# Another assignment of 64 KiB chunks to SBUF partitions in the first tile of a row normalization

## The chip, the cores and the metric

The kernel runs on one core of a Trainium2 chip. The metric is the device time of one execution in microseconds (us), a median over several executions. The record marks every run as fast or slow. All timed runs quoted here are fast ones, at full granted clock, save one single run, whose state is unknown because it was alone. Differences of a few tenths of a microsecond matter in this case, so most experiments were timed in five rounds beside the kernel before, on the same chip (experiments 1 to 8 on one chip, 9 to 12 on another). Figures of single packets and landings come from one profiled execution of each kernel.

## The reference

```python
# x: 1024 x 4096 float32, axis = -1, eps = 1e-12
norm = np.sqrt(np.sum(x ** 2, axis=axis, keepdims=True) + eps)
return (x / norm).astype(np.float32)
```

Each row is divided by its length. The input is 16.78 MB and so is the output.

## The kernel before

The 1024 rows form two tiles of 128 partitions with four rows (64 KiB) each. Each tile has a buffer of its own, so both loads are issued at the start (at 0.0 and 0.8 us). The first load's instruction is moved to the very front of the program. Here is the part that matters:

```python
R = 4
n_tiles = N // (P * R)                                   # 2
x_t   = x.rearrange("(t p r) d -> t p (r d)", p=P, r=R)
out_t = out_flat.rearrange("(t p r) d -> t p (r d)", p=P, r=R)
# ...
for i in range(n_tiles):
    g = RowGroups(nc, io, stats, scratch, D, R, eps_t)
    load = nc.sync.dma_start(out=g.flat(), in_=x_t[i])   # 128 x 64 KiB
    if i == 0:
        first_load_to_front(nc, load.ins)
    groups.append(g)

for i, g in enumerate(groups):
    g.square_dve(R - 1)          # sum of squares of row 3 on VectorE
    g.square_act(0)              # rows 0, 1, 2 on ScalarE
    g.norm(0)
    g.scale(0)                   # VectorE, in place
    # ... rows 1 and 3 ...
    g.square_act(2)
    g.norm(2)
    g.scale(2)
    store = nc.sync.dma_start(out=out_t[i], in_=g.flat())
```

## Time and profile before

| what | value | where it is from |
|---|---|---|
| time before the change was seen | 82.73 us, median of 3 (82.72 to 83.13) | timed runs |
| same kernel beside the later experiments | 82.81 to 82.84 us, medians of 11 or 12 | timed runs |
| VectorE and ScalarE busy | 35% and 33% of the span | page, part 1 |
| DMA engines busy | 97.1% | page, part 3 |
| first load lands, second load lands | 21.89 and 41.89 us | landings in the trace |
| first store issued | 37.88 us | timeline |
| last store lands, span ends | 80.58 and 81.13 us | trace |

The transfers are the bound. Beside the page I use the trace's records of single packets, which give start, duration and size. Every 64 KiB chunk is one packet (512 packets of 65,536 bytes). The records don't name the engine, but nearly every packet starts within 0.004 us of the end of another, which gives 16 chains of 32 packets each; I take each chain for one of the page's 16 DMA engines. Packets 1 to 8 of a chain belong to the first load, 9 to 16 to the second load, 17 to 24 to the first store, 25 to 32 to the second. I call what a packet takes beyond 2.418 us its excess. Two groups of packets have one: the first packet of each engine, and packet 16, the last of the second load.

### The profile page before, as it was taken

What the parts mean: (1) busy time and instruction counts of PE and PEld (TensorE: products, weight loads), DVE (VectorE), ACT (ScalarE), POOL (GpSimd) and SP (SyncE); (2) the same over time, 40 slices, a digit from 0 to 9 for tenths busy, and PEclk for the clock granted to TensorE, in tenths of its full rate; (3) what the DMA queues carried; (4) which work ended last, traced back from release to release, by engine and by line L of the source; (5) the groups of instructions that cost most, each with busy time, mean ns of one, the idle gap of its engine ahead of it and who ended that gap; (6) DMA issues with size and microseconds to landing.
All of it is one profiled execution on the core that took longest, in us unless ns stands there. A gap on an engine that the chain in (4) does not pass through costs nothing.

```text
span 81.1 us, 93 instructions
## 1 busy us (share of the span) xinstructions
DVE 28.6 (35%) x21; ACT 26.4 (33%) x22; POOL 0.2 (0%) x4
## 2 busy tenths in 40 slices
DVE  0000000000199599976039995999200000000000
ACT  6000000000199999930039999950000000000000
POOL 0000000000000000000000000000000000000000
DMA  9099999299999759999099995899998399998390
GB/s 517 0 517 517 517 517 485 129 420 517 517 517 485 323 226 517 517 517 517 0 517 517 517 452 226 355 517 517 517 485 388 162 517 517 517 517 388 162 485 0
DMA packets 577, 33.55 MB, mean 414 GB/s; under 512 B 65, under 2 KB 65, under 8 KB 65
## 3 DMA queue, kind: packets, MB, share of 16 engines
q1 hardware_dynamic: 576, 33.55, 97.1%
q14 instruction: 1, 0.00, 0.0%
HBM read 16.78 MB, written 16.78 MB: 414 GB/s over the span
## 4 chain that ended last, share of the span: by engine, by line
DMA 51%; ACT 10%; DVE 9%; issue 0%
DMA xt<-in_x_dram 51%; ACT sq_act L33 9%; DVE xt L64 9%; ACT rstd L53 1%; DVE rstd L59 0%
## 5 line engine op out<-in xcount | busy, mean ns | idle before, releaser
L33 ACT ACTIVATE sq_act<-xt 128x4096 f32<-128x4096 f32 x6 | 21.6, 3608 | 26.5 <-DMA xt<-in_x_dram 26.5
L64 DVE TENSOR_SCALAR xt<-xt,rstd 128x4096 f32<-128x4096 f32 x8 | 18.8, 2353 | 0.3
L42 DVE SCALAR_TENSOR_TENSOR sq_dve<-xt 128x4096 f32<-128x4096 f32 x2 | 8.9, 4426 | 25.0 <-DMA xt<-in_x_dram 25.0
L53 ACT ACTIVATE rstd<-ssq,eps_t 128x1 f32<-128x1 f32 x8 | 2.1, 288 | 0.1
L59 DVE RECIPROCAL rstd<-rstd 128x1 f32<-128x1 f32 x8 | 1.3, 159 | 2.4 <-ACT rstd L53 2.4
L33 ACT ACT_TABLE_LOAD x1 | 1.3, 1283 | 0.8 <-PEq L220 0.8
L53 ACT ACT_TABLE_LOAD x1 | 1.3, 1283 | 0.0
L33 ACT ACTIVATION_READ_ACCUMULATOR sq_act<-xt 128x1 f32 x6 | 1.1, 186 | 0.0
L176 DVE MEMSET eps_t<- 128x1 f32 x1 | 0.1, 59 | 0.9 <-PEq L220 0.9
L42 DVE DVE_READ_ACCUMULATOR sq_dve<-xt 128x1 f32 x2 | 0.2, 83 | 0.0
L220 POOL MEMSET const-uint8-127<- 128x1 uint8 x1 | 0.1, 102 | 0.0
L220 POOL MEMSET const-bfloat16-1.0<- 128x1 bf16 x1 | 0.1, 101 | 0.0
L220 POOL MEMSET const-float32-0.0<- 128x1 f32 x1 | 0.1, 98 | 0.2 <-issue 0.2
L220 POOL MEMSET const-float32-1.0<- 128x1 f32 x1 | 0.1, 98 | 0.0
## 6 DMA issues: line engine op xcount, KB each, us to landing
xt<-in_x_dram SPq DMA_DIRECT2D x2, 31.5
out_dram<-xt SPq DMA_DIRECT2D x2, 23.3
```

What stands on the lines that cost most here:

```text
L33: self.nc.scalar.activation(out=sq_a, in_=self.x[:, r], func=ACT_F.Square, accum_out=self.ssq[:, r : r + 1],)
L42: self.nc.vector.scalar_tensor_tensor(out=sq_v, in0=self.x[:, r], scalar=1.0, in1=self.x[:, r], op0=ALU.mult, op1=ALU.mult, accum_out=self ...
L53: self.nc.scalar.activation(out=self.rstd[:, r : r + n], in_=self.ssq[:, r : r + n], func=ACT_F.Sqrt, bias=self.eps_t,)
L59: self.nc.vector.reciprocal(out=self.rstd[:, r : r + n], in_=self.rstd[:, r : r + n])
L64: self.nc.vector.tensor_scalar_mul(out=self.x[:, r], in0=self.x[:, r], scalar1=self.rstd[:, r : r + 1])
L176: nc.vector.memset(eps_t, eps)
L220: nc = _bacc.Bacc("TRN2", target_bir_lowering=False, num_devices=1)
```

## The change

The intent, as I read it, is to let the DMA engines read neighbouring 64 KiB chunks of HBM at the same time. Only the first tile is regrouped, load and store alike, so the result is the same; the last tile stays in plain order.

```diff
+    B = 4
+    x_f = x.rearrange("(t b g r) d -> t g b (r d)", b=B, g=P // B, r=R)
+    out_f = out_flat.rearrange("(t b g r) d -> t g b (r d)", b=B, g=P // B, r=R)
+    x_v = [x_f[0]] + [x_t[i] for i in range(1, n_tiles)]
+    out_v = [out_f[0]] + [out_t[i] for i in range(1, n_tiles)]
...
-        load = nc.sync.dma_start(out=g.flat(), in_=x_t[i])
+        load = nc.sync.dma_start(out=g.flat(), in_=x_v[i])
...
-        store = nc.sync.dma_start(out=out_t[i], in_=g.flat())
+        store = nc.sync.dma_start(out=out_v[i], in_=g.flat())
```

## The prediction

> **What bounds the kernel now.** I read the page from the top: the engines' busy time first, the slices of the span next, then the transfer queue, then the chain that ended last, and at last the windows view and the trace's single transfer records.
>
> ```profile
> span 81.1 us, 93 instructions
> DVE 28.6 (35%) x21; ACT 26.4 (33%) x22; POOL 0.2 (0%) x4
> ...
> DMA  9099999299999759999099995899998399998390
> ...
> DMA packets 577, 33.55 MB, mean 414 GB/s; under 512 B 65, under 2 KB 65, under 8 KB 65
> ...
> q1 hardware_dynamic: 576, 33.55, 97.1%
> ```
>
> Both compute engines are busy for about a third of the span, while the transfer queue occupies its 16 DMA engines for 97.1% of it. The low digits in the DMA row are no pauses: packets are long and all 16 engines start them nearly together, so a slice that sees no packet begin shows a low digit. Of the 577 packets 65 are tiny (completion marks and one other), so 512 carry data: 33.55 MB / 512 = 65,536 bytes, one 64 KiB chunk (four rows) for each partition and direction. There are four transfers of 128 chunks (two loads, two stores), so each engine moves 8 chunks of each transfer, 32 in all.
>
> The windows view, cut at the stages, says how fast they go (columns: window, its length, busy time of VectorE, ScalarE and GpSimd, clock, DMA share, GB/s):
>
> ```profile
> 4.60:21.60 17.00, 0.00 (x0) 0.00 (x0) 0.00 (x0) 1.00 1.01 436
> ...
> 36.00:41.90 5.90, 1.85 (x1) 0.00 (x0) 0.00 (x0) 1.00 0.96 378
> 41.90:61.00 19.10, 14.23 (x10) 11.87 (x10) 0.00 (x0) 1.00 1.01 439
> ```
>
> 436 GB/s over 16 engines is 27.25 GB/s each, or 2.41 us for a 64 KiB chunk. The single packet records agree: almost every data packet lasts 2.418 to 2.420 us, loads and stores alike, whether compute runs beside it (41.9 to 61.0) or not (4.6 to 21.6).
>
> The timeline shows why compute does not matter. The loads are issued back to back at the start, the first store at 37.88 us, the second at 57.27:
>
> ```profile
> 37.88 19.73 SPq L202 DMA_DIRECT2D out_dram<-xt  x2
> ```
>
> The second load lands at 41.9, so the first store is already queued behind it; the first store lands at 61.2, so the second is queued behind that one. The DMA engines never wait for compute. The chain of waits on the page follows the compute of the last tile, since it goes back from the last store to the instruction that released it. I do not take it as the bound: that store was released about 4 us before its engines were free.
>
> So the time is one engine's 32 packets in a row plus edges. For the engine that ends last, from the packet records: start at 1.20 us; 32 x 2.418 = 77.38; its first packet takes 3.43 instead of 2.42, an excess of 1.01 (over all engines the first packet lasts 2.64 to 3.43, median 3.1, an excess of about 0.7); packets 14 and 15 add 0.05; packet 16, the last of the second load and the one where loading turns into storing, takes 3.10, an excess of 0.68; neighbouring packets overlap by 0.10 in sum. 1.20 + 77.38 + 1.01 + 0.05 + 0.68 - 0.10 = 80.22 us, and the record says 80.24. The last completion comes at 80.58, the span ends at 81.13, and the timed median is 82.73, 1.6 more than the span.
>
> [...]
>
> **The change part by part.** It alters only which 64 KiB chunk of the first tile lives in which partition. Plainly, partition p holds chunk p. Now partition 4g + b holds chunk 32b + g, in the load and in the store alike, so the result is the same. Nothing is added to the compute engines: the same 43 VectorE and ScalarE instructions on the same shapes, with the same waits.
>
> Packets: the HBM side becomes 32 x 4 chunks instead of 128, still in runs of 64 KiB, so 128 packets for each transfer, 0 more. [...]
>
> [...]
>
> What moves is the HBM address. [...]
>
> What that can be worth: of a tile-0 load's 8 packets, seven already take 2.42 us, and so do all 8 of its store. Only the first packet has any excess, median 0.7 us[...]. If denser addresses save a tenth to a third of it, that is 0.07 to 0.23 us on the path, because the queue behind it moves up by as much. The second load, the turn to storing (0.68) and the second store keep their order: 0. Sum: -0.1 us, 82.73 - 0.1, about 82.6 us.
>
> **The rivals.**
> (1) The split over engines breaks[...]: 8 x 2.42 = 19.3 us more for the load and as much for the store, so 102 to 121 us. [...] I give it 4 in 100.
> (2) HBM suffers from the new addresses[...]. A loss of 2% (1.65 us) needs only 1.65 / 16 = 0.10 us a packet, 4%. [...] I give 4 in 100 to a loss over 2%, and some to a loss of a few tenths.
> (3) The first packets become much quicker: all 16 excesses vanish. That is 0.7 to 1.0 us, 81.7 to 82.0, still within 2%. To pass 2% the change would need 1.65 us, and the slowest engine has 1.74 us of excess in all, 0.73 of it in packets that are not touched.
> (4) The first tile lands earlier and compute starts earlier: worth nothing, since the first store waits in the queue behind the second load anyway.
>
> **Range and chances.** The executions before spread from 82.72 to 83.13. With -0.7 as the good end for the first packets and +0.6 for small losses in HBM, 8 times in 10 I expect 82.1 to 83.3, around 82.6. Slower by over 2%: the rivals 1 and 2 together, 0.08. Faster by over 2%: 0.03, for something I have overlooked. Within 2%: 0.89.
>
> **What would show it.** If right, the profile after has 577 packets and 33.55 MB again, near 436 GB/s between the first packets and the landing of the first load, a first load that lands within 0.5 us of 21.9, a first store issued as much earlier or later, and a span within 0.7 us of 81.1. Rival 1 would show as about 218 GB/s in the windows of the first load and of the first store, rival 2 as packets of 2.5 us or more there, rival 3 as a first load that lands before 21.3. I am wrong if packets of the first tile leave 2.42 us by more than 0.1, or if the second load and second store, untouched, change their time.

The forecast's sum was -0.1 us, 82.73 - 0.1, about 82.6 us. The terms come to -0.1 us: 0.07 to 0.23 us off the measured excess of 0.7, where the fraction, a tenth to a third, was my guess (that the addresses read at one moment become denser was not shown), and zeros for the rest. Of rival 1 an estimate is left, that the first tile's packets take twice their measured 2.42 us.

## The result, and the profile after

The changed kernel takes 83.06 us (median of 6, 82.96 to 83.14); the kernel before, with the runs of the same rounds added, 82.97 us (median of 6, 82.72 to 83.13). The ratio is 1.0013 with a 95% interval of 0.9991 to 1.0035. Ratios throughout are the mean time of one kernel's fast runs over that of the other's fast runs of the same rounds, so they are not quite the ratio of the medians quoted. A difference is not shown. But inside the span two things have moved, by 0.5 to 0.75 us each, in opposite directions.

The page of the changed kernel answers line for line:

```profile
span 81.2 us, 93 instructions
DVE 28.6 (35%) x21; ACT 26.4 (33%) x22; POOL 0.2 (0%) x4
...
DMA packets 576, 33.55 MB, mean 413 GB/s; under 512 B 64, under 2 KB 64, under 8 KB 64
q1 hardware_dynamic: 576, 33.55, 96.4%
```

The work is unchanged, to the instruction and the packet (the one packet less is the instruction fetch that happened to fall into the profile before). The windows view of the changed kernel, same cuts as before, same columns:

```profile
4.60:21.60 17.00, 0.00 (x0) 0.00 (x0) 0.00 (x0) 1.00 1.00 432
...
36.00:41.90 5.90, 2.52 (x2) 0.06 (x1) 0.00 (x0) 1.00 1.18 511
41.90:61.00 19.10, 14.23 (x10) 11.87 (x10) 0.00 (x0) 1.00 1.01 436
```

The steady stages run at the same 432 to 439 GB/s. The view books a packet where it starts, so the middle window must not be read as a rate (511 GB/s are 46 packet starts in 5.9 us, where 39 would fit at 436 GB/s); it does say that something between 36 and 42 us has shifted.

Now the issue, that is, the time that SyncE's instruction takes to hand a transfer over. First the loads, the first store and ScalarE's first work on each tile in the timeline of the kernel before (start, duration, engine or queue, line, operation; the two loads are merged in one line; the lines from 37 us on are from the view cut at 37 to 43 us), then in the changed kernel:

```profile
0.00 1.13 SPq L184 DMA_DIRECT2D xt<-in_x_dram  x2
...
21.91 3.62 ACT L33 ACTIVATE sq_act<-xt 128x4096 f32<-128x4096 f32 x1 [19.83 <-DMA xt<-in_x_dram]
...
37.88 0.35 SPq L202 DMA_DIRECT2D out_dram<-xt  x1
41.91 3.62 ACT L33 ACTIVATE sq_act<-xt 128x4096 f32<-128x4096 f32 x1 [6.64 <-DMA xt<-in_x_dram]
```

```profile
0.00 1.67 SPq L191 DMA_DIRECT2D xt<-in_x_dram  x2
...
22.70 3.62 ACT L33 ACTIVATE sq_act<-xt 128x4096 f32<-128x4096 f32 x1 [20.11 <-DMA xt<-in_x_dram]
...
38.67 0.60 SPq L209 DMA_DIRECT2D out_dram<-xt  x1
42.02 3.62 ACT L33 ACTIVATE sq_act<-xt 128x4096 f32<-128x4096 f32 x1 [5.97 <-DMA xt<-in_x_dram]
```

ScalarE starts on the first tile when it has landed: at 22.70 us instead of 21.91, 0.8 later. Yet the second load lands at 42.00 instead of 41.89. The delay of the first load has all but vanished within the second, which the change did not touch. The tile view shows the cost of one issue, shortest / median / longest in ns, before and after:

```profile
L184 SPq DMA_DIRECT2D xt<-in_x_dram x2: 333/358/383, 0.0 to 0.8; - x2
L202 SPq DMA_DIRECT2D out_dram<-xt x2: 344/346/348, 37.9 to 57.3; - x2
```

```profile
L191 SPq DMA_DIRECT2D xt<-in_x_dram x2: 364/512/660, 0.0 to 1.3; - x2
L209 SPq DMA_DIRECT2D out_dram<-xt x2: 354/479/604, 38.7 to 57.4; - x2
```

Of each pair one is still plain (364 and 354 ns). The regrouped one takes 660 ns for the load and 604 ns for the store, where a plain one takes 0.33 to 0.38 us. Its HBM side now has three dimensions, 32 x 4 x 64 KiB, whose first two have steps that can't be merged into one; that this is the reason is what experiment 9 tests.

The packet records put this together. Means over the 16 engines, us; two profiles of each kernel:

| | before | before, again | changed | changed, again |
|---|---|---|---|---|
| first packet begins | 1.18 | 1.18 | 1.67 | 1.59 |
| first packet lasts | 3.10 | 3.06 | 3.26 | 3.40 |
| first packet ends | 4.28 | 4.24 | 4.94 | 4.99 |
| packets 2 to 8 | 2.42 | 2.42 | 2.42 | 2.42 |
| excess of packet 16 | 0.50 | 0.64 | 0.01 | 0.01 |
| last packet of the slowest engine ends | 80.23 | 80.19 | 80.34 | 80.36 |

In the means over the engines, then, the change costs 0.65 to 0.75 us at the front and gets 0.5 to 0.6 us back where loading turns into storing. The question for the experiments is whether either is chance, what causes each, and whether the gain can be had without the cost.

### The profile page after: what moved, and what is told of

It is laid out like the page before. It is cut to its first block, busy times and chain, and to the rows that moved or that the text cites. A ratio compares the mean times of both kernels' runs of the same rounds, so it can differ in the third digit from the quotient of the medians.

```text
span 81.2 us, 93 instructions
## 1 busy us (share of the span) xinstructions
DVE 28.6 (35%) x21; ACT 26.4 (33%) x22; POOL 0.2 (0%) x4
## 4 chain that ended last, share of the span: by engine, by line
DMA 50%; ACT 10%; DVE 9%; issue 0%
DMA xt<-in_x_dram 50%; ACT sq_act L33 9%; DVE xt L64 9%; ACT rstd L53 1%; DVE rstd L59 0%
```

## The experiments

Two theories. (By the record's verdict, which asks for 2%, every kernel below but the one of experiment 4 is the same as the kernel before. Where I call one slower or quicker, the 95% interval of its ratio leaves 1 out.) **Timing**: packet 16 is long in the kernel before because the first store is issued while the second load is still running, and early; the late start of the changed kernel makes the first tile, and hence that store, later, and the stretch goes away. **Address**: packet 16 is short in the changed kernel because the regrouped order suits HBM better. A third theory, **chance**, says that the long packets were an accident of one execution.

### 1 and 2. Both kernels again, unchanged

> The kernel before, unchanged, as its own control. Theory (the change costs about 0.5 us at the first issue and wins back about 0.5 us where loading turns into storing): the last packets of the second load again take 2.8 us or more, the first packets begin at about 1.0 to 1.6 us, ratio 1.000. Rival (the long last packets of the second load, 2.8 to 3.1 us, are chance of one execution): here they last 2.42 to 2.5 us.

> The changed kernel, unchanged, a second profile. Theory: the first load's issue again takes about 0.5 us longer, the first packets begin at 1.45 us or later, and the last packets of the second load stay at 2.42 to 2.45 us; ratio 1.000 to 1.003. Rival (chance): the last packets of the second load are long here, or the start is as early as before.

The kernel before measured 82.76 us against 82.84 for itself, ratio 0.9993 (0.9978 to 1.0008): this is how well the comparison resolves. The changed kernel measured 83.03, ratio 1.0019 (1.0002 to 1.0037). Together with the first comparison, the change makes the kernel slower by perhaps 0.1 to 0.2%. The table above has both repeat profiles: the stretch of packet 16 and the late start are there again in the respective kernel. Chance alone is out for both. It was right for one thing: packets 13 to 15 of the first profile before had 0.14 us of excess in sum, and none in the second.

### 3. The second tile regrouped instead of the first

```diff
-    x_v = [x_f[0]] + [x_t[i] for i in range(1, n_tiles)]
-    out_v = [out_f[0]] + [out_t[i] for i in range(1, n_tiles)]
+    x_v = [x_t[0], x_f[1]]
+    out_v = [out_t[0], out_f[1]]
```

> The regrouping in the second tile alone (load and store), the first tile plain. If the cost is only the issue of the three-dimensional side: the first packets begin at 1.0 to 1.6 us as before, the longer issue of the second load hides behind the first, and the time is that of before (ratio 0.998 to 1.002), or lower by up to 0.6 us (0.993) if the turn from loading to storing is quick as well. If the new addresses themselves cost time in HBM: packets of the second load or store above 2.5 us, ratio above 1.005.

It measured 82.71 us, ratio 1.0000 (0.9978 to 1.0021). The earliest packet begins at 1.02 us as in the kernel before, and the long issue of the second load (648 ns) costs nothing behind the first load. The packets of the regrouped second load and store are at 2.42 us in the steady state. So regrouping costs when it is the first transfer of the program. Packet 16 had an excess of 0.13 us, between the two kernels, although the first store is plain here and was issued 0.28 us before the mean start of packet 16, nearly as in the kernel before (0.34). Timing alone does not give that. But the profiled execution was the fastest of a scattered lot (82.46 to 83.17), and this run alone does not decide between timing and address.

### 4. Groups of eight partitions

```diff
-    B = 4
+    B = 8
```

> As the change, but 16 groups of eight partitions instead of 32 groups of four. [...] the load and the store of the first tile take up to 19.3 us more each (102 to 121 us in all). Rival: [...] time as before, 83 us.

It measured 124.69 us (one run, state unknown, but the slowest of all other kernels is 41 us faster). The first load lands at 43.38 us instead of 22.68 (+20.7), the first store takes 40.4 us after the second load's landing instead of 19.4 (+21.0), and these 41.7 us are the whole difference from 83.03. The windows view, cut inside the first load and the first store:

```profile
5.00:40.00 35.00, 0.00 (x0) 0.00 (x0) 0.00 (x0) 1.00 1.02 210
64.00:100.00 36.00, 12.85 (x10) 10.49 (x10) 0.00 (x0) 1.00 0.99 213
```

All 16 engines are busy (share 1.02 and 0.99) and move 210 and 213 GB/s, about half of 436. The median packet of the first load takes 5.11 us, and so does that of the first store, where single ones scatter from 3 to 6. This is the breakdown that the prediction's first rival describes, built on purpose, with the rate that it was given (about 218 GB/s). Even its size nearly fits: 5.11 us against 2 x 2.42 = 4.84, 5% more. The 32 groups of the change keep each engine at 2.42 us, so whatever slows the 16 groups isn't there. What that is was not shown: the trace doesn't name the partition of a packet. That the new HBM addresses slow the 16 groups is a possibility which no run excludes; against it stands only that the 32 groups, with new addresses too, stayed at 2.42 us a packet.

### 5 and 6. The load alone, the store alone

Each of these mixes a regrouped and a plain side, so the rows come out in the wrong order.

```diff
# e_load_only
-    out_v = [out_f[0]] + [out_t[i] for i in range(1, n_tiles)]
+    out_v = [out_t[i] for i in range(n_tiles)]
# e_store_only
-    x_v = [x_f[0]] + [x_t[i] for i in range(1, n_tiles)]
+    x_v = [x_t[i] for i in range(n_tiles)]
```

> Only the first load is regrouped, the first store is plain (the rows come out in the wrong order on purpose). Both theories expect the late start: first packets at 1.45 us or later. Timing theory (the last packets of the second load are stretched when the first store is issued well before they end): the store is issued at about 38.65 us and those packets stay under 2.5 us, time as the changed kernel, ratio 1.001 to 1.003. Address theory (they are short because the first store writes regrouped addresses): they take 2.8 us or more here, ratio about 1.007.

> Only the first store is regrouped, the first load is plain (wrong order of rows on purpose). Both: first packets at 1.0 to 1.6 us, store issued at about 37.8 us. Timing theory: the last packets of the second load take 2.6 to 3.1 us, a little less than before [...]; ratio 0.997 to 1.001. Address theory: those packets take 2.42 to 2.45 us, ratio about 0.994.

The load alone measured 83.33 us, ratio 1.0052 (1.0031 to 1.0072), with the first packets at 1.41 us or later and 0.11 us of excess in packet 16 (2.42 to 2.87 us). The store alone measured 82.44, ratio 0.9958 (0.9937 to 0.9978), with an early start and 0.03 us of excess. Its timeline:

```profile
37.88 0.64 SPq L209 DMA_DIRECT2D out_dram<-xt  x1
41.25 3.62 ACT L33 ACTIVATE sq_act<-xt 128x4096 f32<-128x4096 f32 x1 [5.99 <-DMA xt<-in_x_dram]
```

The two halves add up: +0.52% from the load and -0.42% from the store give +0.1%, and the whole change measured 0.13% and 0.19%, with intervals of about 0.2% to either side of each. Each theory missed something. With the load alone the excess is mostly gone although the store is plain, against the address theory; but some packets took over 2.5 us and the ratio lies above the 1.001 to 1.003 of the timing theory. With the store alone it is gone although the store was issued at 37.88 us exactly as before, where the timing theory had expected 2.6 us or more. One way out keeps timing: the regrouped store's issue takes 0.64 us instead of 0.35, so although it begins at 37.88 us as before it ends 0.29 us later. The next two runs were made to tell.

### 7 and 8. The plain store later, the regrouped store earlier

```diff
# b_store_late: the kernel before, result right
         g.scale(2)
+        if i == 0:
+            nc.vector.tensor_scalar_mul(out=g.x[:, 2, :1280],
+                                        in0=g.x[:, 2, :1280], scalar1=1.0)
         store = nc.sync.dma_start(out=out_t[i], in_=g.flat())
# a_store_early: the changed kernel, one row in four of tile 0 wrong on purpose
#   (square_act gets a second argument, the number of columns; that edit is cut here)
-        g.square_act(2)
+        g.square_act(2, 3072 if i == 0 else D)
```

> The kernel before, with one more VectorE multiplication by 1.0 over 1280 columns ahead of the first store alone, about 0.8 us; the result is right. Timing theory: the first store is issued at about 38.6 us, the last packets of the second load shrink from 2.9 to about 2.43 us and the end comes 0.5 us earlier, ratio 0.994. Address theory: those packets stay at 2.8 to 3.1 us and the time stays, ratio 1.000.

> The changed kernel with ScalarE's third square of the first tile cut to 3072 of 4096 columns (one row in four of that tile gets a wrong norm on purpose), so that the first store is issued about 0.85 us earlier, at 37.8 us. Timing theory: the last packets of the second load stretch to 2.7 to 3.1 us and the end comes about 0.3 to 0.5 us later than the changed kernel's, ratio to before 1.006. Address theory: they stay at 2.43 us, ratio 1.001 to 1.003.

The kernel before with a useless multiplication of 0.83 us ahead of its first store measured **82.16 us, ratio 0.9920** (0.9903 to 0.9937), with the right result. The timeline of that kernel:

```profile
37.88 0.83 DVE L203 TENSOR_SCALAR xt<-xt 128x1280 f32<-128x1280 f32 x1
38.73 0.35 SPq L204 DMA_DIRECT2D out_dram<-xt  x1
41.21 3.62 ACT L33 ACTIVATE sq_act<-xt 128x4096 f32<-128x4096 f32 x1 [5.95 <-DMA xt<-in_x_dram]
```

More work on the path to the store, a store issued 0.85 us later, and the second load arrives 0.7 us earlier (41.21 against 41.91), because packet 16 lasts 2.43 us on every engine. No address differs from the kernel before. Conversely the changed kernel with its regrouped store issued at 37.86 us has 0.28 us of excess in packet 16 (2.45 to 3.29 us), its second load lands at 42.67, and it takes 83.55 us (median of 4), ratio 1.0093 (1.0075 to 1.0111), more than the 1.006 that was expected. So timing alone is enough to remove the stretch, and regrouped addresses do not wholly prevent it. The address theory falls as the only cause. It is not shown that the regrouping has no part of its own: 0.28 us is less than the plain store's 0.50 and 0.64, though the regrouped store came earlier against packet 16 (0.86 us before its start; plain 0.34 and 0.39).

### 9. Three dimensions without the regrouping

Tile 0 takes every other group of four chunks and tile 1 the rest. Within a group of partitions the chunks are neighbours as in plain order, but each HBM side is 32 x 4 x 64 KiB as in the change.

```diff
-    x_f = x.rearrange("(t b g r) d -> t g b (r d)", b=B, g=P // B, r=R)
+    x_f = x.rearrange("(g t b r) d -> t g b (r d)", b=B, g=P // B, r=R)
# the output likewise; x_v and out_v are x_f and out_f for both tiles
```

> Tile 0 takes every other group of four chunks, tile 1 the rest, in both loads and stores; within a partition group the four chunks are neighbours as in the plain order, but each HBM side is three-dimensional (32 x 4 x 64 KiB) and can't be merged. If the late start comes from the shape of the transfer's HBM side: first load's issue 0.64 to 0.67 us, first packets from 1.4 us, first load lands at 22.4 or later, although no neighbouring chunks are spread over groups. If it comes from the regrouped addresses: issue 0.33 to 0.38, first packets from 1.0 us, landing by 21.9. In time: with the shape, about as the changed kernel, ratio 1.000 to 1.004; with the addresses, 0.994 to 0.998.

It measured 82.80 us, ratio 0.9995 (0.9977 to 1.0012). The tile view of the loads has both of them long now:

```profile
L191 SPq DMA_DIRECT2D xt<-in_x_dram x2: 564/612/660, 0.0 to 1.3; - x2
```

The first packets begin at 1.58 us in the mean, as in the changed kernel (1.59 and 1.67) and not as before (1.18, and 1.18 to 1.30 in all profiles with a plain first load): the late start of 0.4 to 0.5 us comes from the shape of the transfer, not from spreading neighbouring chunks over groups. But the first packet ends at 4.70 us, against 4.91 to 4.99 in the four profiles with the regrouped first load and 4.24 to 4.45 in those with a plain one, and the first load lands at 22.22 us, not at 22.4 or later as expected. So some 0.2 us of the change's cost may belong to the regrouped addresses of the very first packets. That rests on one profile against four. In time this kernel lies at the lower edge of what the shape was expected to cost (1.000 to 1.004); the excess of its packet 16 is 0.10 us.

### 10 to 12. When should the first store be issued?

```diff
# the kernel before, with the added multiplication over
#   320 columns (b_store_bit_late) or 3712 columns (b_store_too_late);
# b_store_early: g.square_act(2, 3072 if i == 0 else D), wrong on purpose
```

> The kernel before with ScalarE's third square of the first tile cut to 3072 of 4096 columns (a wrong norm in one row of four of that tile, on purpose): the first store is issued at about 37.0 us. Timing theory: the last packets of the second load, or the two last, stretch at least as much as before (mean excess of 0.5 us or more an engine), ratio 1.000 to 1.008. Address theory, already hurt: unchanged.

> The kernel before with an added VectorE multiplication over 320 columns (about 0.25 us) ahead of the first store. Timing theory: issue at about 38.1 us, excess of the last load packets between 0.0 and 0.3 us, ratio 0.992 to 0.997. If only a delay of the best part of a microsecond helps: 1.000.

> The same with 3712 columns (about 2.2 us): issue at about 40.1 us[...]. Timing theory: no stretch of the last load packets, but the store's first packets begin at about 41.1 us on all engines instead of 40.3 to 40.8, so the end comes about 0.4 us later than with the delay of 0.8 us: ratio 0.995 to 1.000. If every later issue helps alike: 0.992.

All three came out as the timing theory expected. They were run on another chip. Together with the earlier runs of the plain kernel they give a curve. Packet 16 begins between 38.05 and 38.22 us (mean over engines) in all of them:

| first store issued at | against the mean start of packet 16 | mean excess of packet 16 | first store packet begins, mean | ratio to before |
|---|---|---|---|---|
| 37.05 (early) | -1.04 | 0.93 | 41.45 | 1.0043 |
| 37.66 (before, again) | -0.39 | 0.64 | 41.11 | 0.9993 |
| 37.88 (before) | -0.34 | 0.50 | 41.15 | |
| 38.16 (a bit late) | +0.04 | 0.16 | 40.70 | 0.9955 |
| 38.73 (late) | +0.65 | 0.01 | 40.53 | 0.9920 |
| 40.25 (too late) | +2.12 | 0.01 | 41.16 | 0.9971 |

The excess falls steadily as the store comes later. The last row is the other end: there the excess is zero, but the engines stand idle for 0.6 us in the mean after packet 16, and all start the store together at 41.10 to 41.30 us. Of these times of issue the best is 0.65 us after the start of packet 16.

The curve holds for the plain kernel. Every kernel with something rearranged in groups of four lies below it. Read off in straight lines between the rows (an estimate), the curve gives 0.47 us at the -0.31 of the store alone and of every other group, which had 0.03 and 0.10; 0.85 at the -0.86 of the regrouped store issued early, which had 0.28; and 0.26 and 0.32 at the -0.07 and -0.14 of the changed kernel's two profiles, which had 0.01. The longer issue of a regrouped store (0.60 to 0.64 us against 0.35) may explain a part of that, which was not tested, but not the two kernels whose first store is plain: 0.13 against 0.45 for the second tile (-0.28), 0.11 against 0.33 for the load alone (-0.15). So the later store accounts for about half of what the changed kernel gains at the turn, by this estimate; the rest goes with the regrouping, and the runs do not say by what way.

## Why the prediction was right or wrong

**Right: the bound.** The transfers set the end in every variant, compute ran in their shadow (save that it sets when the first store is issued, see below), and 83.06 us lies in the range and within 2%.

**Right, as far as the trace shows it: the load on the engines, and the steady rate.** 576 packets, 16 chains of 32 data packets again, 432 to 439 GB/s and 2.42 us a packet in the first tile. The argument for it, which partitions an engine serves, was not shown. The breakdown of rival 1 happens at 16 groups and not at 32, at 41.7 us for the two transfers against the 38.6 estimated. Rival 2, HBM suffering in the steady state, did not come about (2.42 us a packet).

**Wrong: "What that can be worth".** The term was -0.1 us from quicker first packets; it measured +0.65 to +0.75. Two things were missed. The change part by part counted compute instructions ("Nothing is added to the compute engines") and packets ("0 more"), and not the price of issuing a transfer: a transfer with an HBM side that cannot be merged takes 0.28 us longer to issue here and brings the first packets 0.4 to 0.5 us later (experiment 9: the shape alone does it). Since this is the first transfer of the program, that is on the path. And the first packets became longer by 0.16 to 0.34, not shorter.

**Wrong: "The second load, the turn to storing (0.68) and the second store keep their order: 0".** The turn went from 0.50 and 0.64 us of mean excess to 0.01, worth -0.5 to -0.6 us. The prediction had seen the long packets, and named them a part that the change doesn't touch, because their addresses stay. It touches them through time: the first load lands 0.8 us later, so the first store comes 0.8 us later, which is worth about half of the gain by the estimate above. The rest, by the same estimate, goes with the regrouping itself: the regrouped store alone, issued at the same 37.88 us, took the excess to 0.03 us. My own condition for being wrong, that the untouched second load changes its time, was met.

**Wrong: "A first load that lands within 0.5 us of 21.9"** (it landed at 22.68) and, in effect, rival 4. It said that an earlier store is worth nothing since it waits in the queue behind the second load. In fact, in the kernel before, an earlier store costs: 0.43% more time for 0.8 us earlier, 0.8% less for 0.85 us later.

The two wrong terms, about +0.7 and -0.55, nearly cancel. The near agreement of the total with 82.6 us, in a range whose middle it misses, is owed to that and not to the reasoning about the first packets.

**What stays open.** Why a store in the queue stretches a load in progress (by up to 0.93 us in the mean, table above) is not visible in the trace, which gives a packet's start and duration only. Why the kernels with something regrouped lie below the curve of the plain one is open too: what happens between a regrouped store's issue and its first packet was not measured, and it can't be the reason where the first store is plain. Each of these points is one profile. Whether the 0.2 us of longer first packets is a matter of addresses rests on few profiles. Of the 0.4 to 0.5 us of late start the longer issue itself is 0.28; where the rest arises is not shown.

## What to carry to other kernels

When the DMA queue is the bound and always full (97.1% here), look at the edges of it: here the issue of the very first transfer was on the path (0.66 us instead of 0.38, and the first packets 0.4 to 0.5 us later), so try the simplest shape for that one, and more complicated shapes where another transfer hides their issue (in experiment 3 that cost nothing, ratio 1.0000). "As early as possible" was not the best time for a store behind a load on the same engines: moving it from 0.3 us before to 0.65 us after the start of the last load packet was worth 0.8% (0.66 us), about as much as either of the regrouping's two shifts and far more than their sum. And where a change moves nothing in total, compare the landings in order; two opposite shifts show there at once.
